# The FFNs' up-projections of a two-layer macaron decoder, formed by Strassen's seven products

## The chip, the cores and the metric

One NeuronCore of a Trainium2 chip runs the whole program. The metric is device time in microseconds (us) of one execution. TensorE (PE) multiplies; it loads a stationary operand of 128x128 (PEld) and streams a moving operand of up to 512 columns past it into PSUM. VectorE (DVE), ScalarE (ACT) and GpSimd (POOL) work elementwise. SP issues plain DMA transfers, POOL issues transfers that add to what is already in SBUF. Each engine works through its own instructions in a fixed order.

## The reference

Sequence 512, width D = 1024, feed-forward width FF = 2816, two layers, all in float32. A layer has two half-step FFNs around a mixer (convolution, sliding-window attention, attention to 256 memory tokens):

```python
def swiglu(x, w1, w3, w2):
    return (jax.nn.silu(x @ w1) * (x @ w3)) @ w2

for l in range(DEPTH):
    h = x + 0.5 * swiglu(rms_norm(x, ffn1_norm[l]), ffn1_w1[l], ffn1_w3[l], ffn1_w2[l])
    n = rms_norm(h, mix_norm[l]); p = n @ w_in[l]
    ...
    h = h + y @ w_out[l]
    h = h + 0.5 * swiglu(rms_norm(h, ffn2_norm[l]), ffn2_w1[l], ffn2_w3[l], ffn2_w2[l])
    x = rms_norm(h, final_norm[l])
```

So there are four FFNs. Each has two up-projections (512x1024 by 1024x2816, for `w1` and `w3`) and one down-projection (512x2816 by 2816x1024).

## The kernel before

Activations lie transposed: model dimension on partitions in KD = 8 blocks of 128, the 512 tokens along the free dimension. TensorE's fast float32 form rounds its operands, so each operand is split into a rounded part `hi` and a remainder `lo`, and a product is three matmuls (`mm3`, L156 to L159): hi·hi, hi·lo, lo·hi. In a page's rows `mm<-xhi,whi` is a matmul into PSUM tile `mm` with `xhi` moving and `whi` stationary; `cf`, `po` and `pt` are other PSUM tiles.

Weights come as units of up to 128x1024: SP loads `raw` (three buffers, L95), ACT rounds it to `whi` (L131), DVE subtracts to get `wlo` (L132). In the mixer, which keeps DVE busy, `weights(..., G)` has ACT write hi and the negated weights, and POOL adds the weights by a DMA that accumulates (`split_by_dma`, L136 to L138). There are four `whi`/`wlo` pairs.

An FFN works in four quarters of its 22 column blocks. For each block `up` makes two projections of 24 matmuls of 512 columns (w1, then w3), multiplies both by R, takes SiLU and the product, and splits the result into `ghi` and `glo`. R is the reciprocal RMS of each token, spread over partitions by TensorE (`spread`, L195) and copied by ACT (`kept`, L200). The projection itself runs on gain-scaled x without R, so TensorE can begin an FFN before R exists; only DVE's evictions (L249, L251) need it. After the blocks of a quarter, the down-projection adds to the residual `h` for each of eight output blocks (L268). One block of the next quarter is made ahead. In the first FFN of each layer the mixer's memory keys are prepared after the first quarter (`aside`).

A scheduler fixes the order of each engine's instructions when the program is built, and places the buffers; at run time each engine keeps that order and waits on semaphores.

Of the kernel before, what the change touches and what calls it, by code (L numbers as in the profile page):

```python
# [26 lines left out]
NF = FF // P  # L27
QUARTERS = ((0, 6), (6, 6), (12, 5), (17, 5))
CC = 3
# [30 lines left out]
def trunk(ctx: ExitStack, tc: tile.TileContext, xT, memT, pos, w1a, w3a, w2a, w1b, w3b, w2b,  # L60
# [6 lines left out]
    wst = ctx.enter_context(tc.tile_pool(name="wst", bufs=4))  # L67
    gp = ctx.enter_context(tc.tile_pool(name="gp", bufs=8))
    tmp = ctx.enter_context(tc.tile_pool(name="tmp", bufs=4))
# [19 lines left out]

    def sm(n, name, tag="s", bufs=12):  # L90
        return sml.tile([P, 8], F32, tag=tag, name=name, bufs=bufs)[:, 0:n]
# [63 lines left out]

    def mm3(ps, a, b, first, last):  # L156
        T.matmul(ps, a[0], b[0], start=first, stop=False)  # L157
        T.matmul(ps, a[0], b[1], start=False, stop=False)  # L158
        T.matmul(ps, a[1], b[0], start=False, stop=last)  # L159

# [15 lines left out]

    def col_sums(st):

        ss = bank([P, 4], "cf")
        for t in range(st.n // P):  # L180
            for i, x in enumerate(st.sums):
                T.matmul(ss[:, t : t + 1], x[:, blk(t)], onec, start=i == 0, stop=i == len(st.sums) - 1)
        return ss

    def rms_cols(st, width):
        ss, n = col_sums(st), st.n // P
# [53 lines left out]

    def ffn(l, w1, w3, w2, x, R, last, aside=None):
        def up(f):
            pp = []
            for w in (w1, w3):
                ps = mm()
                project(ps, weights(w[l, f], 1024, V), x)
                pp.append(ps)
            u, g = tm("u", "pr", 3), tm("g")
            V.tensor_tensor(out=u, in0=pp[0], in1=R, op=ALU.mult)  # L249
            A.activation(u, u, AF.Silu)  # L250
            V.tensor_tensor(out=g, in0=pp[1], in1=R, op=ALU.mult)  # L251
            V.tensor_tensor(out=g, in0=g, in1=u, op=ALU.mult)
            hi, lo = gp.tile([P, S], F32R, tag="ghi", name="ghi"), gp.tile([P, S], F32R, tag="glo", name="glo")
            split(hi, lo, g, V)
            return hi, lo

        g = {}
        for n, (f0, nf) in enumerate(QUARTERS):
            ahead = 1 if n + 1 < len(QUARTERS) else 0
            for f in range(f0, f0 + nf + ahead):  # L260
                if f not in g:
                    g[f] = up(f)
            for d in range(KD):
                w = weights(w2[l, d, :, f0 * P : (f0 + nf) * P], nf * P, V)
                ps = mm()
                for j in range(nf):
                    mm3(ps, at(w, ALL, blk(j)), g[f0 + j], j == 0, j == nf - 1)
                V.scalar_tensor_tensor(out=h[:, d, :], in0=ps, scalar=0.5, in1=h[:, d, :], op0=ALU.mult, op1=ALU.add)  # L268
                if not ahead:
                    last(d)  # L270
            if aside and not n:
                aside()
# [5 lines left out]
    def rope_tables():  # L278
        n = [P, NT, 32]
        w1, w2 = tm("rope1"), tm("rope2")  # L280
        a, a1, a0, k, r, q, z, ang = (x[:, blk(i)].rearrange("p (t e) -> p t e", t=NT) for x in (w1, w2) for i in range(4))
# [42 lines left out]

    qT = res.tile([P, CC, S], F32, name="qT")
    kz = res.tile([P, 2, S], F32, name="kz")
    qmT = res.tile([P, 2, S], F32, name="qmT")
    vn = res.tile([P, NT, P], F32, name="vn")
    mz = res.tile([P, 2, 2, MEM], F32, name="mz")
    for i in range(2):  # L330
        G.memset(kz[blk(1 - i, HD), i, :], 0.0)
        G.memset(mz[blk(1 - i, HD), :, i, :], 0.0)
    mvn = res.tile([P, 2, 256], F32, name="mvn")
    cv = res.tile([P, CC, S], F32, name="cv")
    rmem = const.tile([P, 2], F32, name="rmem")
# [43 lines left out]
    def memory(l):  # L379

        st = Stat("st", MEM) if l == 0 else None
        pp = [bank([P, S], "po") for _ in range(2)]
        for i in range(2):
# [14 lines left out]
        if st:  # L398
            V.tensor_copy(rmem, rms_cols(st, D))
        for t in range(2):  # L400
            A.activation(mvn[:, t, :], pp[t][:, 256:512], AF.Copy, scale=rmem[:, t : t + 1])
            q = tm("mk")[:, 0:256]
# [4 lines left out]
            pt = to_columns(None, q, 2)  # L407
# [10 lines left out]
    def mixer(l, x, R, rc, last):  # L418
# [3 lines left out]
        sink = rw[:, l, 4 * HD : 4 * HD + NH]  # L422
        y = [(gp.tile([P, S], F32R, tag="ghi", name="yhi"), gp.tile([P, S], F32R, tag="glo", name="ylo")) for _ in range(KD)]


        def conv_in(c):
            pp = []
            for i in range(2):
                ps = mm()
                project(ps, weights(wconv[l, c, i], 1024, G), x)  # L430
                pp.append(ps)
            u, s = ypad[:, c, PAD:], tm("gate", "cv", 2)
            V.tensor_tensor(out=u, in0=pp[0], in1=R, op=ALU.mult)
# [5 lines left out]
        def queries():  # L439
            ww = [weights(wqk[l, i], 1024, G) for i in range(4)]  # L440
            for t in range(NT):
                ps = mm()
                for k in range(KD):
                    mm3(ps, at(x, ALL, k, blk(t)), at(ww[k // 2], ALL, blk(k % 2, 512)), k == 0, k == KD - 1)
                q = tm("q")
                A.activation(q, ps, AF.Copy, scale=rc[:, t : t + 1])
                r = head_scale(ps, rc[:, t : t + 1], 8)
                q2 = tm("q2")
                qv, q2v = (z.rearrange("p (h s e) -> p h s e", s=2, e=32) for z in (q, q2))
# [16 lines left out]
        def values():  # L466
            ww = [weights(wvm[l, i], 768, G) for i in range(4)]
            for t in range(NT):
# [3 lines left out]
                A.activation(vn[:, t, :], ps[:, 256:CCH], AF.Copy, scale=rc[:, t : t + 1])  # L472
                q = tm("mq")[:, 0:256]
                A.activation(q, ps[:, 0:256], AF.Copy, scale=rc[:, t : t + 1])
# [4 lines left out]
        def weighted(c, nk, scores, nm, den, values, po):  # L479

            pr = tm("pr", "pr", 3).rearrange("p (i k) -> p i k", i=2)
            for i in range(2):
# [7 lines left out]
            ptb = tm("ptb", "ptb", 2).rearrange("p (i j q) -> p i j q", i=2, j=2)  # L490
            A.activation(ptb[:, :, 0:nk, :], pt[:, :, 0:nk, :], AF.Copy)
# [4 lines left out]
        def attended(b, c0, c1, po, rd):  # L496

            n = 2 * (c1 - c0)
            z = tmp.tile([P, (c1 - c0) * P], F32, tag=f"yn{c0}", name="yn", bufs=2)
            V.tensor_tensor(out=heads(z), in0=po, in1=rd.unsqueeze(2).to_broadcast([P, n, HD]), op=ALU.mult)  # L500
# [7 lines left out]
        def window(b):  # L508
            nk = 2 if b else 1
            b0, W = b - nk + 1, nk * P  # L510
            nm, es, den, rd = (sm(NH, f"a{n}", "a", 16) for n in range(4))
            po = bank([P, NH, HD], "po")
# [14 lines left out]
        def recall(b):  # L527
            nm, den, rd = (sm(NM, f"m{n}", "a", 16) for n in range(3))
            po = bank([P, NM, HD], "po")
# [17 lines left out]
        def swish():  # L547
            s1 = tm("ln1", "cv", 2)
            G.tensor_tensor(out=s1, in0=cv[:, 0, :], in1=cv[:, 1, :], op=ALU.add)
# [8 lines left out]
            for c in range(CC):  # L558
                s = tm("swish", "cv", 2)
                V.tensor_tensor(out=s, in0=cv[:, c, :], in1=RL, op=ALU.mult)  # L560
# [26 lines left out]
    for d in range(KD):  # L587
        nxt(d)
    R = kept(spread(rms_cols(st, D)), "R")
    for l in range(L):  # L590
        x, st = nxt.x, Stat("st")
# [9 lines left out]

        ffn(l, w1a, w3a, w2a, x, R, into(gn[:, l, N_MIX], (st, None)), lambda: prepare(l))
        rc = const.tile([P, NT], F32, tag="rc", name="rc")
# [3 lines left out]
        mixer(l, nxt.x, R, rc, into(gn[:, l, N_FFN2], (st, None)))  # L607
        R = kept(spread(rms_cols(st, D)), "R")
        st, fin = Stat("st"), gn[:, l, N_FIN]
        if l + 1 < L:  # L610
            st2 = Stat("RL")
            gg = const.tile([P, KD], F32, name="gg")
            V.tensor_tensor(out=gg, in0=fin, in1=gn[:, l + 1, N_FFN1, :], op=ALU.mult)
            ffn(l, w1b, w3b, w2b, nxt.x, R, into(gg, (st, None), (st2, fin)))
            rf = rms_cols(st, D)
# [7 lines left out]
            RF = kept(spread(rf), "RL")  # L623
            for d in range(KD):
                V.scalar_tensor_tensor(out=h[:, d, :], in0=h[:, d, :], scalar=fin[:, d : d + 1], in1=RF, op0=ALU.mult, op1=ALU.mult)
        else:
            def last(d):
                st.add(h[:, d, :], last=d == KD - 1)

            ffn(l, w1b, w3b, w2b, nxt.x, R, last)  # L630
            pr = spread(rms_cols(st, D))
# [61 lines left out]
```

## Time and profile before

| | us |
|---|---|
| three timed runs, median | 1876.4 |
| lowest and highest of them | 1876.38, 1877.34 |
| the profiled execution, its own time | 1880.89 |
| its span, first to last instruction | 1879.1 |
| TensorE, mean granted clock | 0.988 |

The shares of busy time, the rows of single instructions and the waits on which the prediction rests are shown there. A PE row's length includes the pipeline's latency, so rows overlap: the time that a matmul takes from the next is the distance of their starts.

### The profile page before, as it was taken

How to read it: one execution, taken by the hardware profiler on the slowest of the kernel's cores; microseconds unless marked ns; L12 is line 12 of the kernel's file. 1: busy time of each engine (PE TensorE's matmuls, PEld its weight loads, DVE VectorE, ACT ScalarE, POOL GpSimd, SP SyncE). 2: the span in 40 equal slices, each digit the busy share in tenths (PEclk: the TensorE clock that was granted, in tenths of full speed). 3: DMA queues.
4: the chain of work that ended last, by engine and by line, in shares of the span. 5: the costliest groups of instructions: out<-in, count | busy, mean ns of one | idle time of the engine just before them, and what ended most of it. 6: DMA issues, size and time to landing. Idle time of an engine off the chain costs nothing.

```text
span 1879.1 us, 21550 instructions
## 1 busy us (share of the span) xinstructions
PE 1829.9 (97%) x8300; PEld 1508.2 (80%) x8300; DVE 997.0 (53%) x1546; ACT 692.9 (37%) x1119; POOL 142.4 (8%) x144
## 2 busy tenths in 40 slices
PE   8999999999899999999999999999889999999997
PEld 6888888888678888888888888888776788888886
DVE  6474444459936444444654544445589454444444
ACT  4243222355654223222532422225456632222221
POOL 3000000017020000000000000000340200000000
PEclk9999999999999999999999999999989999999998
DMA  5243323276044232323322423234560633323221
GB/s 190 75 152 94 109 80 111 79 182 151 15 100 138 82 119 75 116 73 107 112 81 88 157 76 115 74 106 133 127 143 1 157 102 90 110 82 108 84 90 66
DMA packets 65911, 194.98 MB, mean 104 GB/s; under 512 B 7568, under 2 KB 11920, under 8 KB 65808
## 3 DMA queue, kind: packets, MB, share of 16 engines
q1 hardware_dynamic: 57168, 171.57, 29.1%
q0 software_dynamic: 8640, 22.02, 6.8%
q8 instruction: 66, 1.08, 0.2%
q14 instruction: 37, 0.30, 0.1%
HBM read 191.47 MB, written 2.10 MB: 103 GB/s over the span
## 4 chain that ended last, share of the span: by engine, by line
PE 57%; issue 35%; DVE 3%; DMA 3%; POOL 2%; ACT 1%; SPq 0%; POOLq 0%; DVEq 0%; ACTq 0%
PE mm L158 13%; PE mm L159 13%; PE mm L157 13%; PE cf L157 4%; PE cf L158 4%; PE cf L159 4%; DMA wlo<-in_wout 1%; DVE cv L543 1%; POOL q L452 1%; PE po L494 1%; DMA wlo<-in_wvm 1%; PE pt L489 1%; POOL wlo L138 1%; PE mm L532 1%; DMA wlo<-in_wconv 1%
## 5 line engine op out<-in xcount | busy, mean ns | idle before, releaser
L131 ACT ACTIVATE whi<-raw 128x1024 fp32r<-128x1024 f32 (+2 forms) x312 | 296.1, 951 | 866.9 <-PE mm L158 539.8
L157 PE MATMUL mm<-xhi,whi 128*128 128x512 f32 x1128 | 440.1, 391 | 8.9 <-ACT whi L131 7.2
L159 PE MATMUL mm<-xhi,wlo 128*128 128x512 f32 x1128 | 441.0, 391 | 3.2 <-DMA wlo<-in_wconv 2.4
L158 PE MATMUL mm<-xlo,whi 128*128 128x512 f32 x1128 | 440.7, 391 | 0.2 <-DVE xlo L142 0.2
L132 DVE TENSOR_TENSOR wlo<-raw,whi 128x1024 fp32r<-128x1024 f32 (+2 forms) x312 | 338.9, 1087 | 55.6 <-ACT whi L131 50.7
L157 PEld LDWEIGHTS mm<-xhi,whi 128*128 128x128 f32 x1128 | 212.7, 189 | 53.2 <-ACT whi L131 7.2
L159 PEld LDWEIGHTS mm<-xhi,wlo 128*128 128x128 f32 x1128 | 212.7, 189 | 49.3 <-DMA wlo<-in_wconv 3.2
L158 PEld LDWEIGHTS mm<-xlo,whi 128*128 128x128 f32 x1128 | 212.7, 189 | 45.0 <-DVE xlo L142 1.3
L158 PE MATMUL mm<-glo,whi 128*128 128x512 f32 x528 | 205.4, 389 | 0.0
L157 PE MATMUL mm<-ghi,whi 128*128 128x512 f32 x528 | 205.1, 389 | 0.0
L159 PE MATMUL mm<-ghi,wlo 128*128 128x512 f32 x528 | 205.1, 389 | 0.0
L249 DVE TENSOR_TENSOR u<-mm,R 128x512 f32<-128x512 f32 x88 | 60.7, 691 | 179.0 <-PE mm L159 169.6
L157 PE MATMUL cf<-xhi,whi 128*128 128x512 f32 x376 | 146.7, 390 | 0.3 <-DVE v L619 0.3
L159 PE MATMUL cf<-xhi,wlo 128*128 128x512 f32 x376 | 146.7, 390 | 0.0
L158 PE MATMUL cf<-xlo,whi 128*128 128x512 f32 x376 | 146.4, 389 | 0.0
L268 DVE SCALAR_TENSOR_TENSOR h<-mm,h 128x512 f32<-128x512 f32 x96 | 66.1, 691 | 141.5 <-PE mm L159 141.3
L543 DVE SCALAR_TENSOR_TENSOR cv<-ypad,par,cv 128x512 f32<-128x512 f32 x180 | 131.2, 751 | 0.4
L159 PEld LDWEIGHTS mm<-ghi,wlo 128*128 128x128 f32 x528 | 99.1, 188 | 20.7
L157 PEld LDWEIGHTS mm<-ghi,whi 128*128 128x128 f32 x528 | 99.1, 188 | 20.5
L158 PEld LDWEIGHTS mm<-glo,whi 128*128 128x128 f32 x528 | 99.1, 188 | 20.5
L251 DVE TENSOR_TENSOR g<-mm,R 128x512 f32<-128x512 f32 x44 | 30.4, 691 | 141.5 <-PE mm L159 141.5
L251 DVE TENSOR_TENSOR g<-cf,R 128x512 f32<-128x512 f32 x44 | 30.4, 691 | 138.5 <-PE cf L159 138.4
(217 smaller groups left out, 2275.3 us busy)
## 6 DMA issues: line engine op xcount, KB each, us to landing
raw<-in_w1a SPq DMA_DIRECT2D x44, 512.0 KB, 3.3
raw<-in_w3a SPq DMA_DIRECT2D x44, 512.0 KB, 3.3
raw<-in_w1b SPq DMA_DIRECT2D x44, 512.0 KB, 3.3
raw<-in_w3b SPq DMA_DIRECT2D x44, 512.0 KB, 3.3
raw<-in_w2a SPq DMA_DIRECT2D x32, 384.0 KB, 3.2
raw<-in_w2b SPq DMA_DIRECT2D x32, 384.0 KB, 3.2
raw<-in_w2a SPq DMA_DIRECT2D x32, 320.0 KB, 2.9
raw<-in_w2b SPq DMA_DIRECT2D x32, 320.0 KB, 2.9
```

The costliest lines, as they stand in the source:

```text
L131: A.activation(hi, x, AF.Copy)
L132: on.tensor_tensor(out=lo, in0=x, in1=hi.bitcast(F32), op=ALU.subtract)
L138: G.dma_start(lo, src, accum_op=ALU.add)
L157: T.matmul(ps, a[0], b[0], start=first, stop=False)
L158: T.matmul(ps, a[0], b[1], start=False, stop=False)
L159: T.matmul(ps, a[1], b[0], start=False, stop=last)
L249: V.tensor_tensor(out=u, in0=pp[0], in1=R, op=ALU.mult)
L251: V.tensor_tensor(out=g, in0=pp[1], in1=R, op=ALU.mult)
L268: V.scalar_tensor_tensor(out=h[:, d, :], in0=ps, scalar=0.5, in1=h[:, d, :], op0=ALU.mult, op1=ALU.add)
L452: G.tensor_tensor(out=q2v[:, h0 : h0 + n, half, :], in0=qv[:, h0 : h0 + n, 1 - half, :], in1=sg[:, t, i, half].unsqueeze(1).to_broadcast([ ...
L489: T.transpose(pt[:, i, j, :], pr[:, i, blk(j)], ident)
L543: V.scalar_tensor_tensor(out=cv[:, c, :], in0=ypad[:, c, j : j + S], scalar=conv_w[:, c, j : j + 1], in1=cv[:, c, :], op0=ALU.mult, op1=AL ...
```

## The change

For every pair of column blocks but the first pair of an FFN, each up-projection becomes a 2x2 block product: the weight pair in quarters (two halves of the inner dimension by two column blocks), the normalised activations in quarters (two halves of the inner dimension by 256 tokens). Instead of eight products of quarters, seven are formed, with sums of quarters as operands. A product is 4 blocks of 128 times `mm3` with 256 moving columns.

- `normed` multiplies `h` by gain and R into tiles `n` (L251), now needed before the activation operands can be formed. `Seven.first` and `Seven.rest` make the seven moving operands from `n`: sums `msum` (L280), split into `mh`/`ml` (products 1, 2, 6) and into the buffers of `xhi`/`xlo` (products 3, 5, 7, 4), after the first two blocks are done with these.
- `up_pair` makes a pair of blocks: per matrix two loads of `raw` halves, a tile `wsum` that SP loads (L321) and to which POOL adds a second piece by DMA (L322), and a load `z`. Stationary units in order: `raw` (products 1 and 2), `raw` changed in place by two DVE additions with `wsum` (products 6 and 3), `wsum` (5 and 7), and `z` for both matrices (4). Sums over products go partly through PSUM accumulation and partly through ACT copies (`part`) and DVE additions (L342).
- `msum` and `wsum` share one ring of three buffers, `aux`.
- The first two blocks of an FFN keep `up`; their remainders come by POOL's accumulating DMA (`V if first else G`).
- The quarters are 6, 6, 6 and 4 blocks, with two blocks made ahead. Down-projections use the three `mm` banks alone. To make room, the mixer's tiles share buffers with the new operands, and some rings are shorter.

```diff
-QUARTERS = ((0, 6), (6, 6), (12, 5), (17, 5))
+QUARTERS = ((0, 6), (6, 6), (12, 6), (18, 4))
...
+    def normed(gain, R):
+        n = [gp.tile([P, 2, S], F32, tag=("ghi", "glo")[i % 2], name="n") for i in range(KD // 2)]
+        for k in range(KD):
+            V.scalar_tensor_tensor(out=n[k // 2][:, k % 2], in0=h[:, k, :], scalar=gain[:, k : k + 1], in1=R, op0=ALU.mult, op1=ALU.mult)
+        return n
...
+        def first(self):
...
+            self.plain(1, 0, 0)
+            self.plain(2, 1, 0)
+            f = self.sum((0, 1), (1, 1), ALU.subtract)
+            self.sum(f, (0, 0), ALU.subtract, f)
+            self.cut(6, f)
...
+        def rest(self):
+            far = tuple(x.rearrange("p k (u t) -> p (k u) t", t=QT) for x in operand())
...
+            self.plain(3, 1, 1)
+            self.cut(5, self.sum((0, 0), (0, 1), ALU.subtract))
+            f = self.sum((1, 1), (0, 1), ALU.subtract)
+            self.cut(7, f)
+            self.sum(f, (0, 0), ALU.add, f)
+            self.sum(f, (1, 0), ALU.subtract, f)
+            self.cut(4, f)
...
+    def up_pair(l, w13, f, M):
+        raw = [raw_tile(w13[i][l, f], D) for i in range(2)]
+        X = []
+        for i in range(2):
+            x = wst.tile([P, UNIT], F32, tag="aux", name="wsum", bufs=3)
+            nc.sync.dma_start(x.rearrange("p (f c) -> p f c", f=2), w13[i][l, f : f + 2, :, 0:QW].rearrange("f p c -> p f c"))
+            G.dma_start(x, w13[i][l, f + 1], accum_op=ALU.add)
...
+        def product(ps, w, half, j, first=False):
+            for k in range(4):
+                mm3(ps, at(w, ALL, blk(4 * half + k)), at(M.m[j], ALL, k), first and k == 0, k == 3, skip_group_check=True)
...
+        for i in range(2):
+            w = unit(raw[i])
+            product(xy[i][:, x0], w, 0, 1, first=True)
+            product(xy[i][:, x1], w, 1, 2)
+            A.activation(part[i], xy[i], AF.Copy)
+            add(to[i][:, 0, x0], part[i][:, x0], part[i][:, x1])
+            add(raw[i][:, 0:QW], raw[i][:, 0:QW], X[i][:, QW:])
+            add(raw[i][:, QW:], raw[i][:, QW:], raw[i][:, 0:QW])
+        for i in range(2):
+            w = unit(raw[i])
+            product(xy[i][:, x0], w, 0, 6)
+            A.activation(part[i][:, x1], xy[i][:, x0], AF.Copy)
+            product(zv[i][:, x0], w, 1, 3, first=True)
...
-            ps = mm()
+            ps = bank([P, S], "mm")
...
+        M = Seven(n)
+        M.first()
...
+        for f in range(2):
+            up(f, u[:, f], v[:, f], *g[f])
+        M.rest()
+        if after:
+            after()
```

`after` holds, in the second layer's first FFN, the eight multiplications of `h` by the final gain (L789) that stood ahead of the FFN.

The order that the scheduler made shows three places. First, DVE where the second FFN of layer 0 begins. Before, the row after R is ready evicts block 0 (`mm` is a projection, `R` the spread reciprocal):

```order
L132 TENSOR_TENSOR wlo<-raw,whi 128x1024 x2
L249 TENSOR_TENSOR u<-mm,R 128x512 x2
L251 TENSOR_TENSOR g<-cf,R 128x512
L251 TENSOR_TENSOR g<-mm,R 128x512
L252 TENSOR_TENSOR g<-g,u 128x512
L132 TENSOR_TENSOR wlo<-raw,whi 128x1024
```

After the change, the same place, in three pieces (`n` are the normalised activations, `mh`/`ml` and `xhi`/`xlo` the split moving operands, `msum` their sums):

```order
L251 SCALAR_TENSOR_TENSOR n<-h,gn,R 128x512 x8
L385 TENSOR_TENSOR u<-mm,R 128x512
L387 TENSOR_TENSOR g<-mm,R 128x512
L385 TENSOR_TENSOR u<-mm,R 128x512
L132 TENSOR_TENSOR ml<-n,mh 128x512 x2
L280 TENSOR_TENSOR msum<-n 128x512 x4
L132 TENSOR_TENSOR ml<-n,mh 128x512
L280 TENSOR_TENSOR msum<-n 128x512 x2
L132 TENSOR_TENSOR ml<-n,mh 128x512
L388 TENSOR_TENSOR g<-g,u 128x512
L280 TENSOR_TENSOR msum<-msum,n 128x512 x2
```

The rows go on without a break to the splits that free the first two `aux` buffers (the first `xlo<-msum`, for product 5, and `ml<-msum`, for product 6):

```order
L387 TENSOR_TENSOR g<-mm,R 128x512
L132 TENSOR_TENSOR glo<-g,ghi 128x512
L132 TENSOR_TENSOR xlo<-n,xhi 128x512 x2
L388 TENSOR_TENSOR g<-g,u 128x512
L132 TENSOR_TENSOR xlo<-msum,xhi 128x1024 x2
L132 TENSOR_TENSOR ml<-msum,mh 128x1024
```

Then follow two short additions, `glo`, four more `msum`, and the additions of `wsum` to `raw` whose split is the stationary operand of products 6 and 3:

```order
L342 TENSOR_TENSOR raw<-raw,wsum 128x512
L132 TENSOR_TENSOR xlo<-msum,xhi 128x1024
L342 TENSOR_TENSOR raw<-raw 128x512
L342 TENSOR_TENSOR raw<-raw,wsum 128x512
L342 TENSOR_TENSOR raw<-raw 128x512
L132 TENSOR_TENSOR wlo<-raw,whi 128x1024 x2
L132 TENSOR_TENSOR wlo<-wsum,whi 128x1024 x2
```

What moved: 39 DVE instructions stand between R and the first addition of `wsum`, of which eight (evictions, products with SiLU and splits of the first two blocks) were there before; and the first changed weight unit now waits for both `wsum` tiles. Second, PE at the same place: `L195` spreads R, and 24 matmuls of the first two blocks are left. Before:

```order
L195 MATMUL pt<-cst,rsq_4477 128x128 x3
L159 MATMUL cf<-xhi,wlo 128x512
L157 MATMUL cf<-xhi,whi 128x512
L158 MATMUL cf<-xlo,whi 128x512
L159 MATMUL cf<-xhi,wlo 128x512
```

After the change two matmuls of product 1 (`po<-mh`) stand ahead of those 24, and wait for ACT's `mh`, which is made from `n`:

```order
L195 MATMUL pt<-cst,rsq_5431 128x128 x3
L157 MATMUL po<-mh,whi 128x256 [waits Activation_49]
L157 MATMUL po<-mh,whi 128x256
L157 MATMUL mm<-xhi,whi 128x512 [waits DVE_49]
L158 MATMUL mm<-xlo,whi 128x512
L159 MATMUL mm<-xhi,wlo 128x512 [waits DMASW7_49]
```

So nothing of those 24 can run before the first `mh`. Third, SP's queue there: the loads of `wsum` wait for DVE, and come after the loads of `raw` that wait for ACT alone:

```order
L95 DMA raw<-in_w3b 128x1024 [waits DMAHW3_49,Activation_49]
L326 DMA raw<-in_w1b 128x512 [waits DMAHW4_49,Activation_49]
L326 DMA raw<-in_w3b 128x512
L321 DMA wsum<-in_w1b 128x2x512 [waits DMASW5_49,DVE_49,PE_49]
L321 DMA wsum<-in_w3b 128x2x512 [waits DMASW4_49,DVE_49]
L321 DMA wsum<-in_w1b 128x2x512 [waits DMASW3_49,DVE_49]
```

The DVE instructions waited for are, by their semaphore values, the first `xlo<-msum` above (product 5), `ml<-msum` (product 6) and the later `xlo<-msum` (product 4). Before, SP had nothing there but plain loads of `raw`.

More of the change, by code (lines that the diff above doesn't have):

```diff
@@ L154, in weights, with mm3 @@
         return hi, lo
[L156 to L159, printed above, removed]
+    def mm3(ps, a, b, first, last, **more):
+        T.matmul(ps, a[0], b[0], start=first, stop=False, **more)
+        T.matmul(ps, a[0], b[1], start=False, stop=False, **more)
+        T.matmul(ps, a[1], b[0], start=False, stop=last, **more)
     def at(p, *idx):
@@ L183, in col_sums, with rms_cols @@
         return ss
-    def rms_cols(st, width):
-        ss, n = col_sums(st), st.n // P
+    def rms_cols(st, width, tag="cf"):
+        ss, n = col_sums(st, tag), st.n // P
         v = sm(n, f"ms{n}")
@@ L239, in __call__, with __init__, quarter, sum @@
                 s.add(h[:, d, :], 1.0 if scale is None else scale[:, d : d + 1])
-    def ffn(l, w1, w3, w2, x, R, last, aside=None):
-        def up(f):
+    QW = 512
+    QT = 256
+    def normed(gain, R):
[3 more added lines that the diff above has]
+        return n
+    class Seven:
+        def __init__(self, n):
+            self.n = n
+            self.m = {}
+        def quarter(self, half, i, t):
+            return self.n[2 * half + i][:, :, blk(t, QT)]
+        def first(self):
+            near = (res.tile([P, 3, 4, QT], F32R, tag="nsh", name="mh"), res.tile([P, 3, 4, QT], F32R, tag="nsl", name="ml"))
+            for i, j in enumerate((1, 2, 6)):
+                self.m[j] = at(near, ALL, i)
+            self.plain(1, 0, 0)
[3 more added lines that the diff above has]
+            self.cut(6, f)
+        def sum(self, a, b, op, out=None):
+            out = wst.tile([P, UNIT], F32, tag="aux", name="msum", bufs=3) if out is None else out
+            for i in range(2):
+                z = out[:, blk(i, 512)].rearrange("p (k t) -> p k t", k=2)
+                V.tensor_tensor(out=z, in0=self.quarter(a[0], i, a[1]) if isinstance(a, tuple) else z, in1=self.quarter(b[0], i, b[1]), op=op)
+            return out
+        def plain(self, j, half, t):
+            for i in range(2):
+                hi, lo = at(self.m[j], ALL, blk(i, 2))
+                split(hi, lo, self.quarter(half, i, t), V)
+        def cut(self, j, f):
+            hi, lo = (x.rearrange("p k t -> p (k t)") for x in self.m[j])
+            split(hi, lo, f, V)
+        def rest(self):
+            far = tuple(x.rearrange("p k (u t) -> p (k u) t", t=QT) for x in operand())
+            for i, j in enumerate((3, 5, 7, 4)):
+                self.m[j] = at(far, ALL, blk(i, 4))
+            self.plain(3, 1, 1)
[5 more added lines that the diff above has]
+            self.cut(4, f)
@@ L243, in up, with ffn @@
+    def ffn(l, w13, w2, x, R, n, last, aside=None, after=None):
+        def up(f, u, g, hi, lo):
             pp = []
-            for w in (w1, w3):
-                ps = mm()
-                project(ps, weights(w[l, f], 1024, V), x)
+            for i in range(2):
+                ps = bank([P, S], "mm")
+                project(ps, weights(w13[i][l, f], 1024, V if first else G), x)
                 pp.append(ps)
-            u, g = tm("u", "pr", 3), tm("g")
             V.tensor_tensor(out=u, in0=pp[0], in1=R, op=ALU.mult)
@@ L270, in ffn @@
                     last(d)
-            if aside and not n:
+            if aside and not q:
                 aside()
@@ L279, in rope_tables @@
         n = [P, NT, 32]
-        w1, w2 = tm("rope1"), tm("rope2")
+        w1, w2 = (ypad[:, c, PAD:] for c in range(2))
         a, a1, a0, k, r, q, z, ang = (x[:, blk(i)].rearrange("p (t e) -> p t e", t=NT) for x in (w1, w2) for i in range(4))
@@ L381, in memory @@
         st = Stat("st", MEM) if l == 0 else None
-        pp = [bank([P, S], "po") for _ in range(2)]
+        pp = [bank([P, S], "cf"), bank([P, S], "mm")]
         for i in range(2):
@@ L510, in window @@
             b0, W = b - nk + 1, nk * P
-            nm, es, den, rd = (sm(NH, f"a{n}", "a", 16) for n in range(4))
+            nm, es, den, rd = (sm(NH, f"a{n}", "a", 12) for n in range(4))
             po = bank([P, NH, HD], "po")
@@ L527, in recall @@
         def recall(b):
-            nm, den, rd = (sm(NM, f"m{n}", "a", 16) for n in range(3))
+            nm, den, rd = (sm(NM, f"m{n}", "a", 12) for n in range(3))
             po = bank([P, NM, HD], "po")
@@ L589, in trunk @@
     R = kept(spread(rms_cols(st, D)), "R")
+    n = normed(gn[:, 0, N_FFN1], R)
+    after = None
     for l in range(L):
@@ L623, in trunk, with after @@
             RF = kept(spread(rf), "RL")
-            for d in range(KD):
-                V.scalar_tensor_tensor(out=h[:, d, :], in0=h[:, d, :], scalar=fin[:, d : d + 1], in1=RF, op0=ALU.mult, op1=ALU.mult)
+            n = normed(gg, R)
+            def after():
+                for d in range(KD):
+                    V.scalar_tensor_tensor(out=h[:, d, :], in0=h[:, d, :], scalar=fin[:, d : d + 1], in1=RF, op0=ALU.mult, op1=ALU.mult)
         else:
```

121 lines of the change are left out of this document (87 added, 34 removed).

## The prediction

> **What bounds the kernel now.** I read the page's busy times first, then the rows of the largest groups for their idle time, then the timeline of TensorE for the distance of its starts.
>
> ```profile
> PE 1829.9 (97%) x8300; PEld 1508.2 (80%) x8300; DVE 997.0 (53%) x1546; ACT 692.9 (37%) x1119; POOL 142.4 (8%) x144
> L157 PE MATMUL mm<-xhi,whi 128*128 128x512 f32 x1128 | 440.1, 391 | 8.9 <-ACT whi L131 7.2
> L159 PE MATMUL mm<-xhi,wlo 128*128 128x512 f32 x1128 | 441.0, 391 | 3.2 <-DMA wlo<-in_wconv 2.4
> 600.00:900.00 300.00, 300.00 (x1326) 248.39 (x1325) 134.07 (x164) 82.17 (x101) 0.00 (x0) 1.00 0.31 95
> 200.28 0.39 PE L157 MATMUL mm<-xhi,whi 128*128 128x512 f32 x1
> ...
> 204.81 0.39 PE L159 MATMUL mm<-ghi,wlo 128*128 128x512 f32 x1
> ```
>
> TensorE hardly waits. In 300 us inside FFNs (the windows' row: PE, PEld, DVE, ACT, POOL) it has no gap, DVE works 45% and POOL not at all. Twenty matmuls lie between the last two rows: 4.53 / 20 = **0.2267 us per matmul of 512**. So time falls if TensorE has less to do, as long as no other engine comes late.
>
> **The gain on TensorE.** A pair of blocks takes 2 x 2 x 8 x 3 = 96 matmuls of 512 now, 96 x 0.2267 = 21.76 us. Strassen's form takes 2 x 7 x 4 x 3 = 168 of 256, each with its own weight load. Ten pairs in each of four FFNs make 40. No projection of 256 columns is in the trace, so I look at the nearest widths.
>
> ```profile
> 442.28 0.33 PE L158 MATMUL mm<-wlo,xhi 128*128 128x384 f32 x1
> ...
> 442.97 0.33 PE L159 MATMUL mm<-whi,xlo 128*128 128x384 f32 x1
> 592.57 1.05 PE L195 MATMUL pt<-cst,rsq 128*128 128x128 f32 x8
> 584.82 0.95 PE L182 MATMUL cf<-onesq,st 128*128 128x1 f32 x8
> L182 PE MATMUL cf<-onesq,st 128*128 128x1 f32 x76 | 10.8, 246 | 0.8 <-DVE h L268 0.8
> ```
>
> 384 columns: 0.69 / 4 = 0.173 us. From 384 to 512 that is 0.0537 per 128 columns; carried on, 256 take **0.120 us**, of which some 0.013 do not depend on width. Could the load bind? Eight single-column matmuls, each with a load, take (0.95 - 0.25) / 7 = 0.10 us apiece, so a load fits below 0.120. The other end: eight plain float32 matmuls of 128 columns take (1.05 - 0.30) / 7 = 0.107. The slow far end is 0.173, the row of 384 itself; since the single-column rows speak against a binding load I keep 0.125 as the slow end and 0.107 as the fast one, and take 0.120, to which two rows of the same kind point. A pair then takes 168 x 0.120 = 20.16 us; 40 x (21.76 - 20.16) = **-64 us** (ends -30 and -151). The multiplications fall by an eighth, the time of a pair by only 7%, since the fixed part is paid 168 times.
>
> [...]
>
> **Inside the run of pairs.** DVE's work grows most. Its durations back to back:
>
> ```profile
> 596.57 0.68 DVE L251 TENSOR_TENSOR g<-mm,R 128x512 f32<-128x512 f32 x1
> 597.17 0.68 DVE L252 TENSOR_TENSOR g<-g,u 128x512 f32<-128x512 f32 x1
> 597.77 1.22 DVE L132 TENSOR_TENSOR wlo<-raw,whi 128x1024 fp32r<-128x1024 f32 x1
> 598.90 0.69 DVE L252 TENSOR_TENSOR g<-g,u 128x512 f32<-128x512 f32 x1
> L625 DVE SCALAR_TENSOR_TENSOR h<-h,gn,RL 128x512 f32<-128x512 f32 x8 | 5.4, 744 | 0.0
> L131 ACT ACTIVATE whi<-raw 128x1024 fp32r<-128x1024 f32 x184 | 195.0, 1062 | 511.2 <-PE mm L158 285.2 <-issue 162.1 <-PE cf L158 45.0
> ```
>
> By the starts, 512 columns cost 0.60 us and 1024 cost 1.13. Per pair DVE has eight of 1024 (seven `wlo`, one product), six of 512, four of 256 (half of 0.60 and a little, 0.33) and two scaled ones (0.68): 9.0 + 3.6 + 1.3 + 1.4 = 15.3 us, below 20.16. ACT has 7 x 1.06 and nine shorter copies, some 13 us. Both hide behind TensorE, if the loads keep up:
>
> ```profile
> raw<-in_w1b SPq DMA_DIRECT2D x44, 512.0 KB, 3.3
> wlo<-in_wconv POOLq DMA_DIRECT2D x12, 512.0 KB, 8.7
> wlo<-in_wqk POOLq DMA_DIRECT2D x8, 512.0 KB, 6.8
> ```
>
> A `wsum` needs a free `aux` buffer, 3.3 us of load and then 6.8 to 8.7 us of accumulation. From the split that frees the buffer to the same split one pair on: 3.3 + 8 + DVE's rows between (four of 1024, two of 512, two of 256, 6.4) = 18 us, below 20.16 too. I cost this at 0; uncovered, 1.5 us on the 30 pairs that follow another would be +45.
>
> **Where an FFN begins** the cover is gone. Now R comes late, and nobody minds:
>
> ```profile
> 578.14 0.69 DVE L225 TENSOR_TENSOR st<-st,sq 128x512 f32<-128x512 f32 x1
> 594.29 1.29 DVE L249 TENSOR_TENSOR u<-mm,R 128x512 f32<-128x512 f32 x2 [2.60 <-ACT R L200]
> ```
>
> The sum of squares is done at 578.8; DVE gets R at 594.3, for TensorE reaches the spread (592.57) only after most of the first blocks. In the new order TensorE still has 24 matmuls of 512 behind the spread, then products 1 and 2 of the first pair (48 of 256): 24 x 0.2267 + 48 x 0.120 = 11.2 us, of which 0.75 pass before R is copied. So 10.5 us after R it wants product 6. That needs the changed `raw`, hence both `wsum`, hence two `aux` buffers that hold `msum`. From R on, by DVE's rows: eight `n` 5.4, twenty-one of 512 12.6, product 5's split 1.13: the first buffer is free at 19.1, the second, after two more of 1024, at 21.4. The second `wsum` is complete at 21.4 + 3.3 + 6.8 + 0.3 for hand-overs = 31.8. Two additions (1.2) and the unit's `wlo` (1.13) make it 34.2. **TensorE stands 34.2 - 10.5 = 24 us**; the two hoisted matmuls that wait for `mh` are within this. With DVE's lengths not overlapped (5.95 + 14.5 + 1.23 = 21.7) and 8.7 us of accumulation it is 29; with 5 us of accumulation 22.
>
> The first FFN of all also has the rotary tables among these rows: +2. The second layer's first FFN has the eight `h` rows there (5.4), and its R needs a longer chain with nothing left in front of it (two POOL powers, some 2 us): 31.5. Sum 24 + 24 + 26 + 31.5 = **+106 us** (ends 88 and 128).
>
> **Smaller terms.** After a stall the clock is lower:
>
> ```profile
> 435.24 0.69 PE L158 MATMUL mm<-wlo,xhi 128*128 128x384 f32 x1 [3.03 <-DMA wlo<-in_wvm]
> 436.05 0.52 PE L157 MATMUL mm<-whi,xhi 128*128 128x384 f32 x1
> 436.37 0.52 PE L158 MATMUL mm<-wlo,xhi 128*128 128x384 f32 x1
> 436.00:442.00 6.00, 6.00 (x23) 5.90 (x23) 5.15 (x10) 0.06 (x1) 5.98 (x6) 0.55 1.04 310
> ```
>
> Here 384 columns take 0.32 us instead of 0.173 for six us (granted clock 0.55), which loses about 3. Four times: **+12** (ends 6 and 14). In three FFNs the first blocks' `wlo` comes by an accumulation of 6.8 us or more instead of 1.13 on DVE, and all four pairs of buffers turn over in the eight us before: I take 2 each, **+6** (0 to 15). The last pair of an FFN is needed at once: an addition, a product of 1024, ACT's rounding and hand-overs, 0.4 + 1.2 + 0.6 + 0.4 = 2.6, with about 2 of matmuls left, then the remainder: 1 each, **+4** (0 to 10). The mixer's shorter rings: 0 (-3 to +10), since its instructions stay.
>
> Sum: -64 + 106 + 12 + 6 + 4 = +64. The profiled execution took 1880.9 us, 4.5 over the median of 1876.4 (and 1.8 over its span); 1880.9 + 64 - 4.5 = **1940 us**.
>
> **The rivals.**
> - *The width-free part is not paid at 256.* If the spacing is 0.107 to 0.109, as in the plain float32 row, 40 pairs gain 40 x (21.76 - 18.14) = 145 instead of 64: 1940 - 81 = **1859**, faster. For it: that row. Against: 384 and 512 both carry 0.013. It decides from 0.112 on downward. [...] Chance 0.10.
> - *The FFN's start is covered after all*, the stall some 8 us each: the sum of starts 32, the clock 6 less: 1940 - 80 = **1860**, faster. It would need the `wsum` tiles within about 15 us of R. Against it stand 29 DVE rows and two transfers in series. Chance 0.06.
> - *The pair loop is longer than 20 us*: accumulations slower among 3.5 MB per pair (2 MB now). 1.5 us on 30 pairs: 1940 + 45 = **1985**. For it: 8.7 us where several transfers ran together; against: 20.2 - 15.3 = 4.9 us of slack on DVE. Chance 0.14.
> - *The load binds at 256*, up to the 0.173 of 384 columns: 40 x 168 x 0.053 = 356 more, 2296. Against it the single-column row. Chance 0.02.
>
> **How the numbers follow.** The forecast has 0.68, with a range of its own of 1905 to 1975 from the ends above. To hold 8 in 10 the range reaches to 1858, which takes in the first rival, and to 1990, which takes in the third; the second's middle, the fourth and the tails are left out. Faster by over 0.2% (about what a measurement of this kernel can tell from no change, 4 us): both fast rivals and the forecast's thin edge, 0.17. Within 0.2%: 0.04. Slower: 0.79.
>
> **What would show it.** Starts of `po<-mh` matmuls 0.120 apart, inside pairs; 20.2 us per pair from the second on, without idle time on TensorE. At four places a stall of some 20 us ahead of product 6, released by DVE's `wlo` from `raw`, with DVE itself idle some five us before its addition, waiting for the accumulation. Windows of half clock behind them. Wrong would be: no such stall (then the chain from R is not what I read), or pairs that take 18 or 22 us.

## The result, and the profile after

| | before | after |
|---|---|---|
| median of four runs, us | 1876.87 | 1970.29 |
| lowest and highest | 1876.38, 1877.35 | 1966.84, 1973.28 |
| after over before, with its 95% interval | | 1.0497 (1.0475 to 1.0519) |
| the profiled execution: its time, its span | 1880.89, 1879.1 | 1973.28, 1971.4 |

The change makes the kernel 93 us slower; 64 were forecast. An execution now and then shows a lower granted clock and takes longer (2015.42 us at 0.834 in one case); the times below leave these out. The page of the changed kernel, busy times and two groups:

```profile
PE 1800.5 (91%) x11180; PEld 1613.8 (82%) x11180; DVE 1301.7 (66%) x1972; ACT 939.1 (48%) x1533; POOL 222.2 (11%) x240
L157 PE MATMUL po<-mh,whi 128*128 128x256 f32 x960 | 275.6, 288 | 75.9 <-ACT whi L131 64.4
L132 DVE TENSOR_TENSOR wlo<-raw,whi 128x1024 fp32r<-128x1024 f32 (+2 forms) x338 | 369.9, 1096 | 110.1 <-ACT whi L131 109.5
```

TensorE is busy for less time and idle for more. The row of L157 is the one to see: `po<-mh` opens products 1 and 6, and TensorE stood 64.4 us ahead of it for a `whi`. Inside the run of pairs it does not stand, and its matmuls follow each other as forecast (timeline, and a window of 60 us: PE, PEld, DVE, ACT, POOL, granted clock):

```profile
704.73 0.28 PE L158 MATMUL pt<-xlo,whi 128*128 128x256 f32 x1
...
705.93 0.28 PE L159 MATMUL po<-xhi,wlo 128*128 128x256 f32 x1
700.00:760.00 60.00, 60.00 (x374) 54.34 (x374) 35.37 (x44) 23.11 (x32) 3.45 (x4) 1.00 0.55 151
```

Ten starts between the first and the last row: 1.20 / 10 = 0.120 us. What TensorE waits for in the whole run, longest first (total, times, longest):

```profile
PE po L157 <- ACT whi L131: 64.4, 6, 17.8
PE mm L158 <- DMA wlo<-in_wvm: 14.6, 2, 8.6
PE mm L157 <- DVE u L385: 13.0, 4, 3.4
PE po L157 <- ACT mh L131: 9.1, 4, 2.8
PE mm L159 <- DMA wlo<-in_wconv: 9.0, 5, 2.7
...
PE mm L159 <- DMA wlo<-in_w1b: 5.7, 2, 2.9
PE mm L159 <- DMA wlo<-in_w1a: 5.0, 2, 3.2
PE mm L157 <- ACT ghi L374: 4.8, 4, 1.5
```

The first row is four stalls of 14.5 to 17.8 us, one at each FFN's start, and two short waits behind them. The same view of the kernel before has 1.7 us for a bank (`DVE u`, there L249) and, of the transfers, only

```profile
PE mm L158 <- DMA wlo<-in_wvm: 9.5, 2, 6.4
PE mm L159 <- DMA wlo<-in_wconv: 2.4, 1, 2.4
```

To see where the 92 us between the two spans lie, I cut both traces at the last addition to `h` of each FFN and mixer, and compared the distance between consecutive matmuls of `mm3` with columns / 2.4 + 13.5 ns. This is a line through the spacings at full clock: 227 at 512 columns in both traces, 173 at 384 before, 120 at 256 after. Distances of up to 2.3 times that count as a slow clock, longer ones as waits.

| us | before | after | difference | forecast |
|---|---|---|---|---|
| four FFNs: matmuls at full clock | 1456.1 | 1395.0 | -61 | -64 |
| four FFNs: waits, and what lies around R's spread | 21.9 | 141.6 | +120 | +116 |
| four FFNs: slow clock | 3.1 | 23.5 | +20 | +12 |
| two mixers, all of it | 381.8 | 396.1 | +14 | 0 |
| end | 16.3 | 15.3 | -1 | 0 |

The chain at the start of layer 0's second FFN (timelines of DVE, SP's queue, POOL and TensorE; R is there at 618.65):

```profile
618.65 5.39 DVE L251 SCALAR_TENSOR_TENSOR n<-h,gn,R 128x512 f32<-128x512 f32 x8 [3.10 <-ACT R L200]
...
636.58 2.36 DVE L132 TENSOR_TENSOR xlo<-msum,xhi 128x1024 fp32r<-128x1024 f32 x2
638.85 1.22 DVE L132 TENSOR_TENSOR ml<-msum,mh 128x1024 fp32r<-128x1024 f32 x1
...
637.87 0.38 SPq L321 DMA_DIRECT2D wsum<-in_w1b  x1
640.10 0.38 SPq L321 DMA_DIRECT2D wsum<-in_w3b  x1
...
642.40 0.93 POOL L322 DMA_DIRECT2D wsum<-in_w1b  x1 [27.23 <-DVE msum L280]
645.14 0.86 POOL L322 DMA_DIRECT2D wsum<-in_w3b  x1 [1.82 <-DMA wsum<-in_w3b]
...
649.02 0.69 DVE L342 TENSOR_TENSOR raw<-raw,wsum 128x512 f32<-128x512 f32 x1 [5.26 <-DMA wsum<-in_w1b]
...
650.76 0.69 DVE L342 TENSOR_TENSOR raw<-raw 128x512 f32<-128x512 f32 x1
652.23 0.69 DVE L342 TENSOR_TENSOR raw<-raw,wsum 128x512 f32<-128x512 f32 x1 [0.79 <-DMA wsum<-in_w3b]
...
651.48 1.06 ACT L131 ACTIVATE whi<-raw 128x1024 fp32r<-128x1024 f32 x1 [6.63 <-DVE raw L342]
...
652.59 0.58 PE L157 MATMUL po<-mh,whi 128*128 128x256 f32 x1 [14.50 <-ACT whi L131]
...
654.80 0.58 PE L157 MATMUL po<-mh,whi 128*128 128x256 f32 x1 [0.99 <-ACT whi L131]
```

Two tiles run through these rows, one behind the other. The first: `xlo<-msum` frees its buffer at 637.81, SP issues the first `wsum` at 637.87, POOL its accumulation at 642.40, DVE adds it at 649.02 and 650.76, ACT rounds the changed unit at 651.48, and TensorE begins product 6 at 652.59. The second: `ml<-msum` ends at 640.07 and SP issues the second `wsum` 0.03 later; POOL issues its accumulation at 645.14; DVE uses it at 652.23, and TensorE, which can do four matmuls of product 6 and 3 without it, waits for the unit made from it until 654.80. So the long stall ends with the first `wsum`. The clock behind the waits, by windows:

```profile
624.70:629.40 4.70, 4.70 (x11) 3.73 (x12) 4.70 (x9) 1.23 (x3) 0.00 (x0) 0.51 0.00 0
652.60:660.00 7.40, 6.41 (x28) 6.12 (x29) 5.64 (x6) 3.34 (x4) 0.86 (x1) 0.50 0.65 178
```

The granted clock there is 0.51 for 4.7 us and 0.50 for 7.4 us; the second stretch has the short wait until 654.80 in it.

### The profile page after: what moved, and what is told of

Same layout as the page of the kernel before. It is cut to its first block, busy times and chain, and to the rows that moved or that the text cites. A ratio compares the mean times of both kernels' runs of the same rounds, so it can differ in the third digit from the quotient of the medians.

```text
span 1971.4 us, 28919 instructions
## 1 busy us (share of the span) xinstructions
PE 1800.5 (91%) x11180; PEld 1613.8 (82%) x11180; DVE 1301.7 (66%) x1972; ACT 939.1 (48%) x1533; POOL 222.2 (11%) x240
## 4 chain that ended last, share of the span: by engine, by line
PE 63%; issue 12%; DVE 11%; DMA 10%; POOL 2%; ACT 2%; POOLq 0%; SPq 0%; DVEq 0%; ACTq 0%
PE mm L159 9%; PE mm L157 9%; PE mm L158 9%; PE po L157 6%; PE po L159 6%; PE po L158 6%; PE pt L159 5%; PE pt L158 5%; PE pt L157 5%; DMA wsum<-in_w3a 2%; DMA wsum<-in_w3b 2%; DVE there L701 2%; DMA wlo<-in_wconv 1%; DVE msum L280 1%; DVE n L251 1%
## 5 line engine op out<-in xcount | busy, mean ns | idle before, releaser
L157 PE MATMUL po<-mh,whi 128*128 128x256 f32 x960 | 275.6, 288 | 75.9 <-ACT whi L131 64.4
L157 PE MATMUL mm<-ghi,whi 128*128 128x512 f32 x752 | 290.2, 392 | 5.6 <-ACT ghi L374 4.8
L159 PE MATMUL po<-mh,wlo 128*128 128x256 f32 x960 | 273.7, 285 | 1.6 <-DVE wlo L132 1.6
L157 PE MATMUL pt<-xhi,whi 128*128 128x256 f32 x960 | 273.2, 285 | 1.0 <-DVE u L342 0.5
L158 PE MATMUL po<-ml,whi 128*128 128x256 f32 x960 | 273.6, 286 | 0.0
L158 PE MATMUL pt<-xlo,whi 128*128 128x256 f32 x960 | 272.9, 284 | 0.0
L159 PE MATMUL pt<-xhi,wlo 128*128 128x256 f32 x960 | 272.3, 284 | 0.0
L157 PEld LDWEIGHTS po<-mh,whi 128*128 128x128 f32 x960 | 186.4, 195 | 79.5 <-ACT whi L131 65.8
L159 PEld LDWEIGHTS po<-mh,wlo 128*128 128x128 f32 x960 | 186.3, 194 | 2.4 <-DVE wlo L132 2.2
L157 PEld LDWEIGHTS pt<-xhi,whi 128*128 128x128 f32 x960 | 185.9, 194 | 2.8 <-issue 0.7
L158 PEld LDWEIGHTS po<-ml,whi 128*128 128x128 f32 x960 | 186.6, 194 | 0.6
L157 PEld LDWEIGHTS mm<-ghi,whi 128*128 128x128 f32 x752 | 140.9, 188 | 36.7 <-ACT ghi L374 6.6
```

What stands on the lines that cost most here:

```text
L157: T.matmul(ps, a[0], b[0], start=first, stop=False, **more)
L158: T.matmul(ps, a[0], b[1], start=False, stop=False, **more)
L159: T.matmul(ps, a[1], b[0], start=False, stop=last, **more)
```

## The experiments

Each is a change to the changed kernel, except the last. Unless said otherwise the times are medians, to be held against 1970.3.

**All blocks by eight products**, with the rest of the change left in place:

```diff
-        M = Seven(n)
-        M.first()
...
-                    g[f], g[f + 1] = up_pair(l, w13, f, M)
+                    g[f], g[f + 1] = gated()
...
+                        up(f + i, u[:, i], v[:, i], *g[f + i])
```

> All blocks formed by eight products; the seven products and their operands (n, msum, mh, ml, wsum) are gone, everything else of the change stays (quarters 6, 6, 6, 4, three banks, first two blocks' remainders by accumulating DMA, the mixer's shared buffers and shorter rings). Theory: what the layout costs is the mixers' 14 us and, at three FFN starts, a wait of 3 us for a DMA-fed remainder with 1.7 us of half clock behind it (14 together), so 1876.9 + 28 = about 1905. Rival: the mixers became longer because of the seven operands, whose buffers they share; then 1877 to 1890.

Measured: 1936.0, ratio 1.032 (1.030 to 1.035). Both expectations missed: without one Strassen product the kernel is 60 us slower than before. By the cuts, the mixers take 13 more than before (5.7 and 7.0), the second FFNs 5.7 each, the first FFNs 12.7 and 15.3 (the cuts are of single executions, which lie 51 apart where the medians lie 60 apart). TensorE's waits in this kernel:

```profile
PE mm L158 <- DMA wlo<-in_wvm: 12.8, 2, 7.6
PE mm L510 <- DVE hv L482: 8.2, 2, 4.7
PE mm L159 <- DMA wlo<-in_wconv: 7.1, 4, 2.7
...
PE mm L159 <- DMA wlo<-in_w1b: 5.2, 2, 2.9
PE mm L510 <- DVE ypad L542: 4.9, 2, 2.6
```

The `mm L510` rows (transposes of the memory keys, 13.1 us) are this kernel's own; the changed kernel has no such wait. The rows of the accumulated weights stand in the changed kernel's list too. So by the medians some 47 us are lost here, beside the 13.1, without any product being formed. That the changed kernel loses all of the 47 is not shown; the mixers' share is nearly the same there (14), so it does not come from the products.

**The first pair's `wsum` ahead of `msum`**, so that the transfers wait for no split:

```diff
+        X = wsums(l, w13, FIRST)
         M = Seven(n)
         M.first()
```

> The first pair's two wsum tiles are allocated, loaded and accumulated ahead of the msum tiles, so the transfers no longer wait for DVE's cuts; msum is left with one buffer until a wsum comes free. Theory (chain R, n, msum cuts, aux free, load, accumulation, changed raw): product 6 then waits only for its own ml, some 20.5 us after R, and product 5 some 5 us more; the stall falls from 25 to about 16 us, with some half clock less, four times: about 1930. Rival: DVE's rows behind R set the stall and the transfers lie beside them: 1965 to 1970. Second rival: the one msum buffer is what is late next: 1950 to 1970.

Measured: 1925.9, ratio 1.027 (1.025 to 1.029), 44 us less: the first theory's number. The wait for `whi` ahead of `po<-mh` is gone; what is left of this kind (the first row is the second pair's):

```profile
PE po L160 <- DVE wlo L133: 9.9, 2, 5.3
PE mm L158 <- DVE u L390: 9.8, 3, 3.4
PE po L158 <- ACT mh L132: 8.9, 3, 3.8
```

**Operands without R** (the seven products are formed from `h` times gain alone):

```diff
-            V.scalar_tensor_tensor(out=n[k // 2][:, k % 2], in0=h[:, k, :], scalar=gain[:, k : k + 1], in1=R, op0=ALU.mult, op1=ALU.mult)
+            V.tensor_scalar(out=n[k // 2][:, k % 2], in0=h[:, k, :], scalar1=gain[:, k : k + 1], scalar2=None, op0=ALU.mult)
```

> The n tiles are h times gain without R (R is left out of the seven products' operands; the first two blocks keep it). They can be made as soon as each h block is there, some 16 to 20 us before R. Theory: the whole chain moves ahead by that, product 6's operands are there when TensorE comes, three quarters or more of the four stalls and of their half clock go: 1870 to 1890. Rival: what counts is DVE's work at that place, which stays; it only moves against the mixer's end: 1920 to 1945. Second rival: R is not in the chain: 1970.

Measured: 1951.0, ratio 1.040 (1.038 to 1.042), 19 less: none of the three. TensorE's waits still begin with

```profile
PE po L157 <- ACT whi L131: 53.6, 6, 13.8
```

At the same FFN, by the timelines of SP's queue, TensorE and DVE:

```profile
610.04 0.38 SPq L321 DMA_DIRECT2D wsum<-in_w1b  x1
637.52 0.38 SPq L321 DMA_DIRECT2D wsum<-in_w3b  x1
...
633.01 0.39 PE L159 MATMUL mm<-xhi,wlo 128*128 128x512 f32 x1
...
636.24 2.35 DVE L132 TENSOR_TENSOR xlo<-msum,xhi 128x1024 fp32r<-128x1024 f32 x2
...
647.65 0.69 DVE L342 TENSOR_TENSOR raw<-raw,wsum 128x512 f32<-128x512 f32 x1 [3.70 <-DMA wsum<-in_w3b]
```

The first `wsum` is loaded at 610, while TensorE is still at the first blocks; the second waits until 637.5 for a buffer whose split writes `xlo`. The first blocks use `xhi` and `xlo` up to the matmul at 633.0, whatever R does. So R is only one of two conditions behind the same buffer, and the ring of three is the knot.

**The first blocks' remainders by DVE** (`V if first else G` becomes `V`):

> The first two blocks' remainders by DVE instead of an accumulating DMA. Theory: the waits of 2 to 3 us at three FFN starts, each with half clock behind it, go: 3 x 4.7 = 14 less, 1956. Rival: the R chain sets the start anyway and DVE's eight extra subtractions (1.1 us each) lie in it: 1970 to 1978.

Measured: 1949.4, ratio 1.039 (1.037 to 1.041), 21 less, where 14 were expected; by the cuts both first FFNs take 6 us less, the second ones 3.6 and 6.7. With **both edits**:

> The first pair's wsum ahead of msum and the first blocks' remainders by DVE, both. Theory: they are two separate costs, 44 and 21 us, so 1970 - 65 = 1905 (1898 to 1912). Rival: both only make room at the same FFN start, DVE being the limit there: 1918 to 1926.

Measured: 1908.6, ratio 1.017 (1.016 to 1.019). 44 + 21 = 65 was expected, 62 came: two nearly separate costs.

**Four blocks by eight products first**, with both edits (`for f in range(2)` becomes a loop over four):

> As the kernel with both edits, and four blocks instead of two by eight products first: 96 matmuls of 512 columns, 21.8 us, more for TensorE behind R; four pairs fewer by seven products cost 4 x 1.5 = 6. Theory: the remaining stalls of some 13 us at each FFN start and 2 to 4 of half clock are covered: 1905 - 60 + 6 = about 1851, below the kernel before. Rival: products 3, 5, 7, 4 have their operands in xhi and xlo, which now come free 21.8 us later, so the stall moves to them, 5 to 8 us each: 1872 to 1885.

Measured: 1903.8, ratio 1.016 (1.013 to 1.019): only 5 less than with two blocks, near neither number. The stalls at product 6 are gone, but others stand in their place:

```profile
PE mm L158 <- DVE u L390: 19.4, 3, 7.2
...
PE mm L158 <- ACT mh L132: 6.8, 1, 6.8
```

TensorE fills three `mm` banks, and their evictions stand behind eight rows of `n` in DVE's order. **The same cover without moving `wsum`:**

> Four blocks by eight products first and remainders by DVE, but the wsum tiles stay behind the msum tiles in the ring. Theory: one aux buffer comes free only by the split for product 5, which writes xhi and xlo and so waits for the last matmul of the first blocks, some 27 us after R; the second wsum is complete some 13 us later, and TensorE, which comes to product 6 at 33 us, still waits some 12 us: 1949 - 44 + 6 = about 1911. Rival: cover alone counts, the ring does not: 1850 to 1865, like the kernel with wsum first.

Measured: 1940.8, ratio 1.034 (1.033 to 1.036), 30 above the expectation. Its waits:

```profile
PE po L157 <- ACT whi L131: 37.4, 4, 11.3
PE mm L157 <- DVE u L385: 19.4, 3, 7.2
```

The stall of 12 us is there, somewhat shorter (8.3 to 11.3); the 19.4 us for the banks, which the number had left out, come on top. Cover alone is not what counts: the 37 us by which this kernel is slower than the one before it are about those of the first row, which that one does not have.

**The additions of `msum` on GpSimd**, with both edits and two blocks:

```diff
-                V.tensor_tensor(out=z, in0=self.quarter(a[0], i, a[1]) if isinstance(a, tuple) else z, in1=self.quarter(b[0], i, b[1]), op=op)
+                G.tensor_tensor(out=z, in0=self.quarter(a[0], i, a[1]) if isinstance(a, tuple) else z, in1=self.quarter(b[0], i, b[1]), op=op)
```

> As the kernel with both edits (two blocks first), with the twelve msum additions of each FFN on GpSimd. Theory: with the transfers out of the way DVE's rows behind R are the limit; 12 x 0.6 = 7 us fewer rows, 4 to 6 us of stall less at each FFN start: 1905 - 20 = 1885. Rival: GpSimd takes 1.4 us for 512 columns (its row of squares), 17 us in series, and is later than DVE was: 1905 to 1925.

Measured: 1916.4, ratio 1.022 (1.020 to 1.023): the rival, 8 us more. What the trace shows of the reason is told at the end.

**Evictions ahead of `n`, and four banks:**

```diff
+            if f == 2:
+                M = Seven(normed(*n))
+                M.first()
...
-                ps = bank([P, S], "mm")
+                ps = mm()
```

> As the kernel with four blocks first, but n is made after the first two blocks' evictions in DVE's order, and the first blocks use four banks instead of three. Theory: what is left at the FFN starts is TensorE standing 5 to 7 us behind the spread, because its three banks wait for evictions that stand behind eight rows of n (5.4 us); with 3 us of half clock behind each that is 4 x 8 = 30 of 1904: about 1875, level with the kernel before. Rival: the operands of product 1 and 6 come as much later as n is moved back: 1892 to 1904.

Measured: 1899.3, ratio 1.013 (1.011 to 1.014): 4 less, not 30. That is the rival's number, but not for its reason: the bank waits went, and the stall moved on to product 6 of the second pair, whose `wsum` waits for a buffer of the first. **Two of the four value weights by DVE** on top (`V if i < 2 else G`):

> The same with two of the four value weights (wvm) of each mixer split by DVE instead of an accumulating DMA. Theory: TensorE's waits of 5 and 8 us for that remainder go, with some half clock: 12 to 18 less than the kernel with evictions first, about 1860. Rival: DVE is 18 of 20 us busy there and the rows behind are late in turn: no change within 4 us.

Measured: 1886.4, ratio 1.0055 (1.0040 to 1.0070): 13 less, as the theory had it (its 1860 counted on the 30 above). What then leads TensorE's waits, and one of them on the timeline:

```profile
PE po L160 <- DVE wlo L133: 22.6, 4, 6.4
...
649.70 0.58 PE L160 MATMUL po<-mh,wlo 128*128 128x256 f32 x1 [6.07 <-DVE wlo L133]
```

**`msum` out of the ring** (into `ypad`, idle in an FFN), and four convolution weights by DVE:

```diff
-            out = wst.tile([P, UNIT], F32, tag="aux", name="msum", bufs=3) if out is None else out
+            out = ypad[:, 0:2, PAD:] if out is None else out
...
-                project(ps, weights(wconv[l, c, i], 1024, G), x)
+                project(ps, weights(wconv[l, c, i], 1024, V if c < 2 else G), x)
```

> As the kernel with the value weights by DVE, with two edits: msum is kept in ypad, which is idle in an FFN, so that the third aux buffer is free for the second pair's first wsum; and the first four convolution weights of each mixer are split by DVE too. Theory: the stall that moved to the second pair (5 to 6.5 us at product 6, with 6.8 us of half clock behind it) goes at all four FFN starts, 4 x 9 = 36, and some 6 us of waits for wconv remainders: 1886 - 42 = about 1845, below the kernel before. Rival: DVE's rows are what is late there, the transfer only the last of them: 1872 to 1886.

Measured: **1863.9**, ratio 0.9935 (0.9921 to 0.9948): 22.5 less where 42 were expected, more than the rival allowed, and faster than the kernel before by 12 us.

**The kernel before with the two mixer edits alone**, to tell whose gain that is:

> The kernel before, with the two mixer edits alone (two of four wvm and four of six wconv weights per mixer split by DVE), to tell what of the gain belongs to the seven products. Theory: its waits for those remainders (3.0, 2.4 and 6.4 us, with half clock behind them) go: about 1862. Rival: DVE is nearly full there and the rows behind are late: 1877 within 4.

Measured: 1878.5, ratio 1.0011 (1.0000 to 1.0022): the rival. So the mixer edits by themselves do not give the 12 us that the last version is ahead of the kernel before; against before, its four FFNs take 16.6 us less and its mixers 3.8 (cuts as above, of two executions that lie 21 apart where the medians lie 12 apart, so rather too much). Of the 36 pairs' 57.6 us (36 x 1.6), some 40 or more are thus still given back inside the FFNs.

## Why the prediction was right, and where its sizes were not

*The gain.* Right: 0.120 us at 256 columns, no idle inside pairs, 61 us for the 64 of the sum. The rival in which the width-free part is not paid fell with it, and the one in which the load binds.

*The pair loop.* Right at 0: from the second pair on no wait worth naming, though accumulations land in 7.2 to 8.2 us.

*The FFN's start.* Right in the chain, wrong in its last link, and somewhat too large. As forecast, `xlo<-msum` frees the first buffer 19.2 us after R and `ml<-msum` the second 21.4 after it, the transfers follow in series, and DVE stands 5.26 us for an accumulation. But the 34.2 us were added up for the second `wsum` and the `wlo` of the changed unit. Product 6 begins 33.9 us after R on the first `wsum`: its first matmuls need only `whi`, which ACT rounds as soon as that tile is added. The second `wsum` is complete at 33.6 (31.8 forecast) and lets TensorE go on at 36.2. So it is luck that 33.9 and 34.2 lie so close. That the first changed unit waits for both tiles, as was said ahead of the prediction, holds for its `wlo` in DVE's order and not for its `whi`.

In the order of time the four starts have product 6 at 33.5, 33.9, 37.4 and 34.3 us after R, in each before the unit from the second `wsum` is there. Less the prediction's 10.5 us of matmuls that is 23.0 + 23.4 + 26.9 + 23.8 = 97, where 106 were forecast; the 2 us for the rotary tables do not show. Moving the transfers out of the chain takes 44 us away. The 24 matmuls behind the spread also wait 3.4 us for a bank (`DVE u L385`), which lies inside the same stall and adds nothing. What the prediction did not see is that R is not the only condition: without it the buffer waits for `xlo`.

*The clock.* The table's 20 for 12 are not all this term's. By the distances between matmuls, the four FFNs of the changed kernel lose 8.8 us at a slow clock behind the start of product 6, which is what the term was for. Another 6.7 are lost between R and product 6, behind the waits for `mh` and for a bank; they lie inside the 97, since DVE's rows and the transfers set when product 6 begins. And 8.0 are lost ahead of R, where the kernel before loses 2.8: the waits for the first blocks' weights are there. After two of the waits, TensorE works on without another from 624.70 and from 654.80, and the half clock lasts 4.7 and 5.2 us.

*DMA-fed weights of the first blocks.* Mis-sized: 6 forecast, 21 by the run that takes them away; in the changed kernel's trace 10.7 are waits for them (`in_w1b`, `in_w1a`) and 5.2 are the added slow clock ahead of R. Where the last five lie is open. A range of 0 to 15 did not hold it.

*The ends.* 4 forecast, 4.8 found.

*The mixers.* Mis-sized, one of the two largest misses: 0 forecast "since its instructions stay", 14 found; the kernel without any product has 13 of them. The waits that grew are those for accumulated remainders (`wvm` 9.5 to 14.6, `wconv` 2.4 to 9.0). Instructions had stayed, their buffers had not. The accumulations of `wvm` also take longer from issue to landing, 10.9 us where it was 7.1 (medians of eight); those of `wconv` do not (8.6 for 8.7). Which of the shared rings makes them late was not tried.

The sum thus came out 30 low, with misses of both signs. Too low were the mixers by 14, the first blocks by 10 to 15, the gain by 3 and the ends by 1; too high were the starts by 9 and the clock behind them by some 4. What is left, 10 to 15 us, was not followed one by one; the trace has waits behind product 6 that no term named, the longest 1.6, 1.4 and 1.0 us, for a `wlo`, a copy by ACT and the second changed unit.

## What to carry to other kernels

An algorithm with fewer multiplications pays per matmul the part that does not depend on width (here 13.5 ns of 120 at 256 columns, by the line through the spacings), and once per stage the time until its operands exist; here the four starts cost 97 us where the products save 61, and the fixes moved the wait on: to the next `wsum` of the same ring, or to a bank. Where sums of operands and sums of weights share buffers, follow the buffer, not the operand: it linked a transfer to an elementwise chain that had no data in common with it. And when a change shortens rings elsewhere "to make room", run the old algorithm in the new layout first: here that alone was 60 us slower, 13 of them in a wait that only this version has.

## What the runs showed of the hardware

With `msum` on GpSimd, DVE itself slowed down. Timeline of that kernel, POOL and DVE:

```profile
610.38 3.62 POOL L281 TENSOR_TENSOR msum<-n 128x512 f32<-128x512 f32 x2 [7.36 <-DVE n L252]
613.97 3.40 POOL L281 TENSOR_TENSOR msum<-msum,n 128x512 f32<-128x512 f32 x2
...
612.15 0.68 DVE L392 TENSOR_TENSOR g<-mm,R 128x512 f32<-128x512 f32 x1
613.34 1.22 DVE L133 TENSOR_TENSOR ml<-n,mh 128x512 fp32r<-128x512 f32 x1
614.48 3.44 DVE L133 TENSOR_TENSOR ml<-n,mh 128x512 fp32r<-128x512 f32 x2
...
618.45 0.68 DVE L393 TENSOR_TENSOR g<-g,u 128x512 f32<-128x512 f32 x1
```

POOL adds from 610.38 to 617.37. In that time `ml<-n,mh`, with two inputs from SBUF, takes DVE 1.22 us and then 3.44 / 2 = 1.72 each, where the sixteen of the changed kernel, in which DVE makes `msum` itself, take 0.68 to 0.69; `g<-g,u`, also with two, takes 0.68 once POOL has stopped, and a row with an input in PSUM (`g<-mm,R`) keeps its 0.68 in the middle of it. POOL takes 1.7 to 1.8 us for an addition in these rows instead of the 1.4 that was expected from its row of squares, whose mean is 1.40 in the changed kernel and 1.51 in this one. Why the one row is slower and the other is not, the trace does not show. How much of the 8 us comes from DVE's slower rows and how much from POOL's own was not separated.
